# Queries reversed within each block so that bias tiles come from one row per head, a quad's sixth weight split placed behind a bank's copy, and the last four squares spaced

## The chip, the cores and the metric

The kernel runs on one core of a Trainium2 chip. The metric is the device time of one execution in microseconds. Before the change it is 1312.29 us, the median of three runs (1311.63 to 1313.32). The core's engines run side by side: TensorE (PE) multiplies matrices, with the loading of its stationary operand shown apart as PEld; VectorE (DVE) and ScalarE (ACT) do arithmetic on tiles; GpSimd (POOL) does a little arithmetic and issues DMAs that add into their target; SyncE (SP) issues most of the other DMAs. A name such as ACTq or SPq in the profile stands for the instructions by which an engine issues DMAs or waits.

## The reference, cut to what matters

One decoder layer on 512 rows of 1024 numbers: a feed-forward network (FFN), a mixer with an SSD part and a differential-attention part, cross attention into 256 memory rows, a second FFN, and a last norm.

```python
x = x + 0.5 * swiglu(rms_norm(x, norm_ffn1_w), ffn1_w_in, ffn1_w_out)     # d_ff = 2816
x = x + hybrid_mixer(rms_norm(x, norm_mix_w), ...)
x = x + memory_cross_attention(rms_norm(x, norm_cross_w), rms_norm(mem, norm_mem_w), ...)
x = x + 0.5 * swiglu(rms_norm(x, norm_ffn2_w), ffn2_w_in, ffn2_w_out)
return rms_norm(x, norm_final_w)

# in the mixer, for each of 8 attention heads and each block of 128 queries:
rel = k_pos[None, :] - q_pos[:, None]
bias = rel_bias[rel_bucket(rel)]            # depends on the distance alone
logits = einsum(q_blk, k) * scale + bias    # two maps, c = 0 and 1
logits = where(rel <= 0, logits, -inf)
w = softmax(logits[c=0]) - lam * softmax(logits[c=1])
out = w @ v
```

The bias of a query and a key depends only on their distance, so a head has one row of 512 biases, followed by masked places.

## The kernel before, in words

All large products are made in a form that keeps float32 accuracy: each operand is cut into a high part (a copy on ACT, line 155, output `wh` for weights) and a low part (a subtraction on DVE, line 156, output `wl`), and a product is three matmuls, high by high, high by low and low by high.

The two FFNs use a Strassen-like scheme. A *quad* (`quad`, line 252) makes a block of the hidden layer from seven weights, called here by their names in the code, in the order in which they are used: m1, t, t2, m2, m7, m3, t4. Each weight meets one combination of the activations in a product of 24 matmuls. The products go to three PSUM banks: "11" to `qa`, S1 to `qe`, S2 to `qb` (on top of a copy of `qa`), "12" to `qa`, S3 to `qb`, S4 to `qe`, "22" to `qb`. Between S2 and S3 the bank `qb` has to be read: line 302 copies it to `u` on ACT, and line 303 subtracts `u` from `qe` on DVE. S3 can't write the bank before the copy has read it. The quad's results are then turned into a gate (lines 450 to 453: a multiplication by the norm's `row`, a sigmoid-like function on ACT, two products into `th`).

FFN1 and FFN2 each run in thirds, of 6, 8 and 8 blocks of hidden columns (two blocks to a quad). In the second and third third of FFN1 there are eight quads whose weights t2 and t4 are summed on DVE (lines 297 and 300) while t and m7 are summed by a POOL DMA that adds into the tile (line 251). The eleven quads of FFN2 take sums that were made earlier in DRAM. The first quad of FFN2 is `fresh`: the last part of its activations arrives late, so its first two products are done in another order. After each third, `out_blocks` multiplies the `th` results by the second weight matrix into three pairs of banks (`oa`, `oe`, `ob`, matmuls of line 1300). In FFN1 its weights, too, are sums: first t1 is fetched by SP (line 1281) and added to by POOL (line 1320), then t2 = t1 + a fetched tile on DVE (line 1330), and so on. Two of the sums of the last third go into a spare tile named `gate`.

Weight tiles sit in rings: six for the fetched weights (`wr`), three each for `wh` and `wl`, four PSUM banks for the products. A fetch can start when the tile it will overwrite has been read.

The order of work has three layers. The code is emitted by an `Order` object, which holds a clock (`od.t`, advanced by each matmul), the dense work, and chains that are started at given clock values. SP and POOL then run their instructions in the order of the code. PE, ACT and DVE are reordered by a scheduler in the framework, which places an instruction by its own forecast of times; `with behind([ins]):` tells it that what is issued inside must come after a given instruction.

Between the FFNs lies the middle of the kernel. For each of the eight attention heads `queries_keys` projects queries into a bank `pq` (512 columns, one for each query) and splits them (`split("q", ...)`, lines 159 and 160, outputs `qh` and `ql`), does the same for the keys, and asks for the head's bias tile one head ahead (`ask_bias`, line 738). `scores` multiplies queries by keys and adds the bias in one DVE operation (line 776). At the end of a head, its output is transposed into a bank `pot` and split to `yah` and `yal`, with a multiplication by `wsub`; `out_attn` reads these later.

The bias tile is 128 x 512: its row p must be the head's bias row, moved by p places. Before the change the kernel writes for each head an expanded copy in DRAM, `rel_z` (128 rows of 641, 320 KB), by `expand_bias` (line 640; two on ACT's queue in `prepare`, six on SP's queue in `queries_keys`), and reads the tile from it with a step of 640, one less than a row.

Ahead of FFN2, `turn(0)` and `turn(1)` transpose the activations, copying eight tiles on ACT. Each tile is also squared and summed on ACT (`squared`, line 554). `row_from` makes the norm's row from the eight sums, by small operations on DVE and POOL and a matmul. The gate of a quad needs that row; its matmuls don't.

Of the kernel before, what the change touches and what calls it, by code (L numbers as in the profile page):

```python
# [11 lines left out]
F32 = mybir.dt.float32  # L12
# [88 lines left out]
def body(tc, a, dbg=None):  # L101
# [130 lines left out]
    def add_product(ps, w, xs, which, first, ks=None):  # L232

        wh, wl = w
        n = len(xs)
        for f in range(2):
            out = ps[:, f * H : (f + 1) * H]
            for kp in ks or range(n):
                wc = slice((f * n + kp) * P, (f * n + kp + 1) * P)
                xh, xl = xs[kp][which]  # L240
                for j, (a_, b_) in enumerate(((wh, xh), (wh, xl), (wl, xh))):
                    od.t += (H + 32) / 2400
                    newest_mm[:] = [nc.tensor.matmul(out, a_[:, wc], b_, start=first and f == 0 and kp == 0 and j == 0, stop=kp == n - 1 and j == 2, skip_group_check=True).ins]  # L243
                yield
# [15 lines left out]
    def quad(xs, src, ready, fresh=False):  # L260
# [38 lines left out]
        if not ready:  # L299
            V.tensor_tensor(t4, t2, m2, ALU.add)  # L300
        u2 = s2("u2")
        S.activation(u2, b_ps, AF.Copy)  # L302
        V.tensor_tensor(e_ps, e_ps, u2, ALU.subtract)
        yield from add_product(a_ps, split_w(m2), xs, "12", False)
        w7 = split_w(m7)
# [2 lines left out]
        yield from add_product(b_ps, w7, xs, S3, False)  # L308
        c22 = s2("c22")
        V.tensor_tensor(c22, p5, b_ps, ALU.subtract)  # L310
        yield from add_product(e_ps, split_w(m3), xs, S4, False)
        yield from add_product(b_ps, split_w(t4), xs, "22", False)
        yield (a_ps, b_ps), (e_ps, c22)

# [279 lines left out]
    wsub = cp.tile([P, 1], F32, name="wsub")  # L594
    dskh = cp.tile([P, 8], F32, name="dskh")
    rel_d = dram.tile([8, RW], F32, name="rel_d")
    rel_z = dram.tile([8, P, RW + 1], F32, name="rel_z")

    def lambdas():
        lamv = cp.tile([P, 4, 64], F32, name="lamv")  # L600
# [16 lines left out]
    def prepare():  # L617
        rel_far = small("rel_far", 64, bufs=1)[:8]
        V.memset(rel_far, MASKED)
        yield 9.0  # L620
        prel = aux("prel", (8, T))
        for i in range(2):
            mm(prel[:, i * H : (i + 1) * H], rel_sb, hot[i], True, True)
        for c in range(T, RW, 64):
            S.dma_start(rel_d[:, c : c + 64], rel_far)
        yield 1.5
        for i in range(2):
            S.activation(hot[i][:8], prel[:, i * H : (i + 1) * H], AF.Copy, scale=-8.0)
        yield 2.0
        for i in range(2):  # L630
            S.dma_start(rel_d[:, i * H : (i + 1) * H], hot[i][:8])
        hot.clear()
        yield 6.0
        for hd in range(2):
            with behind(list(recent)):
                expand_bias(S, hd)
            yield 4.0

    def expand_bias(queue, hd):
        queue.dma_start(rel_z[hd, :, :RW], rel_d[hd : hd + 1].to_broadcast([P, RW]))  # L640

    def bc_c(t):
        return t[:, None, :].to_broadcast([P, 4, 16])
# [91 lines left out]

    def ask_bias(hd):
        biases[hd] = s2("bias")
        S.dma_start(biases[hd], bass.AP(rel_z.tensor, rel_z.offset + hd * P * (RW + 1) + P - 1, [[RW, P], [1, T]]))

    def queries_keys(hd):  # L740
        if hd == 0:
            ask_bias(0)
        if hd < 7:
            ask_bias(hd + 1)
        if hd < 6:
            expand_bias(nc.sync, hd + 2)
        pq = acc("pq")
        yield from proj(pq, load_w(a["wq"][hd]), h)
        q = split("q", pq, -1.0)
        pk = acc("pk")  # L750
        yield from proj(pk, load_w(a["wk"][hd]), h)
        kq = split("k", pk)
        od.spawn(head(hd, q, kq, biases.pop(hd)), W["h0"])

    def head(hd, q, kq, bias):
# [92 lines left out]
        pt = aux("pot")  # L848
        for b in range(4):
            transpose(pt[:, b * P : (b + 1) * P], on[:, b])  # L850
        ya[hd] = split("ya", pt, wsub)
        dump(f"ya_{hd}", ya[hd][0])

    wcv = []
# [607 lines left out]
            yield from out_blocks(a[f"f2b{c}"], wsum[c], g, col4, ncol4, *((norm, store) if at_end else (None, None)), clean=c == 0)  # L1462

    def turn_last():
        yield from turn(1, summed=True)
        od.spawn(row_from(st_2, 8.0), 3.0)

    od.add(turn_last())
    od.add(ffn2())
# [89 lines left out]
```

## Time and profile before

| | |
|---|---|
| median of three runs | 1312.29 us (1311.63 to 1313.32) |
| the profiled execution | 1312.46 us |
| its span, first to last instruction | 1310.7 us (1.8 us lie outside it) |
| PE busy | 1287.7 us (98%), 7709 matmuls |
| DVE busy | 970.1 us (74%) |
| ACT busy | 707.8 us (54%) |
| POOL busy | 127.1 us (10%) |
| mean granted TensorE clock | 0.998 of full speed |
| moved by DMA | 237.38 MB, mean 181 GB/s |

Busy time is the sum of an engine's instruction times. A row of a timeline gives the start in the span, the duration, the engine, the line, the operation, the output and its inputs with their sizes; what stands in brackets is how long the engine had been idle before, and what ended the idling. In the view of waits a row reads: engine, its output and line, what it waited for; then the sum, the number of times and the longest. The duration of a matmul is drawn to a modelled end, so pace is better read from the starts: inside a quad's product the 24 matmuls start 0.12 us apart, 2.88 us for a product.

### The profile page before, as it was taken

The page shows a single profiled execution, that of the slowest core. Times are in us where ns is not written, and L with a number is a line of the kernel's source. Part 1 is how long each engine was busy: PE and PEld are TensorE (multiplying, and loading weights), DVE is VectorE, ACT ScalarE, POOL GpSimd, SP SyncE. Part 2 cuts the span into 40 slices and gives each one's busy share as a digit, 9 for nine tenths or more (in the row PEclk, how much of TensorE's full clock was granted, in tenths as well). Part 3 has the DMA queues.
Part 4 walks back from the last instruction along what each step waited for, and adds up shares of the span by engine and source line. Part 5 has one row for each costly group of instructions (what it writes and reads, how often), then busy time and mean ns, then how long its engine had stood idle before and what let it go on. Part 6 is the DMA issues. An engine that isn't in the chain of part 4 may idle for free.

```text
span 1310.7 us, 20079 instructions
## 1 busy us (share of the span) xinstructions
PE 1287.7 (98%) x7709; PEld 1123.3 (86%) x7709; DVE 970.1 (74%) x1538; ACT 707.8 (54%) x1208; POOL 127.1 (10%) x153
## 2 busy tenths in 40 slices
PE   9999999999999999999999999999999999999997
PEld 7879998997787778777788878888889999989995
DVE  6977897797775676557867686645668878877886
ACT  7545564565754564346645465434365646555564
POOL 0001010001010011101003022020001000000000
PEclk9999999999999999999999999999999999999999
DMA  9367777776984434763466548684139876656652
GB/s 339 94 171 182 203 192 212 223 200 187 291 294 146 137 65 131 256 171 105 92 185 174 177 138 239 191 222 126 66 100 272 207 232 179 189 194 180 188 200 94
DMA packets 70415, 237.38 MB, mean 181 GB/s; under 512 B 8288, under 2 KB 9792, under 8 KB 69968
## 3 DMA queue, kind: packets, MB, share of 16 engines
q1 hardware_dynamic: 54064, 182.87, 41.1%
q0 software_dynamic: 13168, 45.67, 19.4%
q10 hardware_dynamic: 3088, 7.56, 1.6%
q8 instruction: 60, 0.98, 0.3%
q14 instruction: 35, 0.29, 0.1%
HBM read 233.92 MB, written 50.91 MB: 217 GB/s over the span
## 4 chain that ended last, share of the span: by engine, by line
PE 59%; issue 11%; DVE 3%; ACT 2%; DMA 1%; POOL 1%; POOLq 0%; ACTq 0%; DVEq 0%
PE pm L146 10%; PE qb L243 8%; PE qe L243 5%; PE qa L243 5%; PE pxbc L146 4%; PE ob L1300 4%; PE pcq L146 3%; PE pz L146 3%; PE oe L1300 2%; PE oa L1300 2%; PE pcv L146 2%; PE pq L146 2%; PE pv L146 1%; PE pk L146 1%; DMA gate<-in_f1b 1%
## 5 line engine op out<-in xcount | busy, mean ns | idle before, releaser
L155 ACT ACTIVATE wh<-wr 128x1024 fp32r<-128x1024 f32 (+1 forms) x323 | 328.4, 1020 | 355.7 <-issue 75.6
L156 DVE TENSOR_TENSOR wl<-wr,wh 128x1024 fp32r<-128x1024 f32 (+1 forms) x323 | 377.8, 1173 | 142.4 <-ACT wh L155 136.1
L777 ACT ACTIVATE ec<-ec,mn 128x512 f32<-128x512 f32 (+3 forms) x64 | 35.3, 554 | 33.7 <-DVE mn L776 33.7
L146 PE MATMUL pxbc<-hnh,wh 128*128 128x512 f32 x128 | 52.6, 411 | 0.0
L146 PE MATMUL pxbc<-hnh,wl 128*128 128x512 f32 x128 | 50.2, 393 | 0.0
L146 PE MATMUL pxbc<-hnl,wh 128*128 128x512 f32 x128 | 50.2, 392 | 0.0
L243 PE MATMUL qb<-s31h,wh 128*128 128x256 f32 x152 | 43.2, 284 | 3.2 <-ACT u L302 3.2
L243 PE MATMUL qb<-s24h,wh 128*128 128x256 f32 x152 | 43.1, 284 | 1.3 <-ACT qb L287 1.3
L243 PE MATMUL qa<-h11h,wh 128*128 128x256 f32 x152 | 43.1, 283 | 0.0
L243 PE MATMUL qa<-hmh,wh 128*128 128x256 f32 x152 | 43.0, 283 | 0.0
L243 PE MATMUL qa<-hml,wh 128*128 128x256 f32 x152 | 43.0, 283 | 0.0
L243 PE MATMUL qe<-s24h,wh 128*128 128x256 f32 x152 | 43.0, 283 | 0.0
L243 PE MATMUL qe<-s24l,wh 128*128 128x256 f32 x152 | 43.0, 283 | 0.0
L243 PE MATMUL qe<-s24h,wl 128*128 128x256 f32 x152 | 43.0, 283 | 0.0
L243 PE MATMUL qb<-hmh,wh 128*128 128x256 f32 x152 | 43.0, 283 | 0.0
L243 PE MATMUL qb<-hml,wh 128*128 128x256 f32 x152 | 43.0, 283 | 0.0
L243 PE MATMUL qb<-hmh,wl 128*128 128x256 f32 x152 | 43.0, 283 | 0.0
L243 PE MATMUL qa<-h11h,wl 128*128 128x256 f32 x152 | 43.0, 283 | 0.0
L243 PE MATMUL qb<-s24l,wh 128*128 128x256 f32 x152 | 43.0, 283 | 0.0
L243 PE MATMUL qb<-s24h,wl 128*128 128x256 f32 x152 | 43.0, 283 | 0.0
L243 PE MATMUL qa<-h11l,wh 128*128 128x256 f32 x152 | 43.0, 283 | 0.0
L243 PE MATMUL qa<-hmh,wl 128*128 128x256 f32 x152 | 43.0, 283 | 0.0
(457 smaller groups left out, 4169.9 us busy)
## 6 DMA issues: line engine op xcount, KB each, us to landing
wr<-in_f2q SPq DMA_DIRECT2D x44, 512.0 KB, 4.3
wr<-in_f1q SPq DMA_DIRECT2D x40, 512.0 KB, 4.4
wr<-in_f1b SPq DMA_DIRECT2D x25, 512.0 KB, 5.3
isum<-in_f2q SPq DMA_DIRECT2D x22, 512.0 KB, 5.2
wr<-isum SPq DMA_DIRECT2D x22, 512.0 KB, 5.1
wsum<-in_f2b SPq DMA_DIRECT2D x20, 512.0 KB, 6.2
wr<-wsum SPq DMA_DIRECT2D x20, 512.0 KB, 4.7
wr<-in_f1q POOLq DMA_DIRECT2D x16, 512.0 KB, 5.9
```

The lines of the kernel that those rows point to most:

```text
L146: newest_mm[:] = [nc.tensor.matmul(out, w, x, start=start, stop=stop).ins]
L155: S.activation(hi, src, AF.Copy),
L156: V.tensor_tensor(lo, src, hi.bitcast(F32), ALU.subtract),
L243: newest_mm[:] = [nc.tensor.matmul(out, a_[:, wc], b_, start=first and f == 0 and kp == 0 and j == 0, stop=kp == n - 1 and j == 2, skip_gr ...
L777: S.activation(ec[:, :n], ec[:, :n], AF.Exp, bias=mn, scale=-1.0, accum_out=sm[c][:, i : i + 1])
L1300: newest_mm[:] = [nc.tensor.matmul(ps, a_[:, ts], b_[:, ws], start=first and k == 0 and j == 0, stop=k == n - 1 and j == 2, skip_group_che ...
```

## The change

There are three parts.

**The bias.** The expanded copy `rel_z` and its eight DMAs go. The bias tile is read from the head's single row in DRAM, with a step of one place from row to row (pattern `[[1, P], [1, T]]`). That gives the rows in the opposite order, so that the queries have to be reversed within each block of 128. This is done where the query bank is read to be split: `backwards` reads each block of 128 columns from its end to its start (a step of -1), on ACT for the high part and on DVE for the low part. The head's output then comes out reversed as well, and is put right where the bank `pot` is read to be split into `ya`, in the same way. For eight heads these are 16 reads on ACT and 16 on DVE.

**The sixth weight.** In `quad` the split of m3 is issued behind the copy of bank `qb` to `u`.

**The last squares.** `turn(1)` no longer squares its tiles. A chain of its own, `row_of_last`, started 4.0 on the clock after, issues the four squares 2.0 apart, each behind the weight split that was issued last, and then goes on to `row_from`, with 3.0 in place of 8.0 between its steps.

```diff
@@ quad
         u2 = s2("u2")
-        S.activation(u2, b_ps, AF.Copy)
+        copy = S.activation(u2, b_ps, AF.Copy)
         V.tensor_tensor(e_ps, e_ps, u2, ALU.subtract)
...
-        yield from add_product(e_ps, split_w(m3), xs, S4, False)
+        with behind([copy.ins]):
+            w3 = split_w(m3)
+        yield from add_product(e_ps, w3, xs, S4, False)
@@ prepare, queries_keys, head
-    rel_z = dram.tile([8, P, RW + 1], F32, name="rel_z")
...
-        yield 6.0
-        for hd in range(2):
-            with behind(list(recent)):
-                expand_bias(S, hd)
-            yield 4.0
-
-    def expand_bias(queue, hd):
-        queue.dma_start(rel_z[hd, :, :RW], rel_d[hd : hd + 1].to_broadcast([P, RW]))
...
-        S.dma_start(biases[hd], bass.AP(rel_z.tensor, rel_z.offset + hd * P * (RW + 1) + P - 1, [[RW, P], [1, T]]))
+        S.dma_start(biases[hd], bass.AP(rel_d.tensor, rel_d.offset + hd * RW, [[1, P], [1, T]]))
+
+    def backwards(t):
+        n = t.free_size()
+        return bass.AP(t.tensor, t.offset + P - 1, [list(t.ap[0]), [P, n // P], [-1, P]])
...
-        if hd < 6:
-            expand_bias(nc.sync, hd + 2)
...
-        q = split("q", pq, -1.0)
+        q = split("q", backwards(pq), -1.0)
...
-        ya[hd] = split("ya", pt, wsub)
+        ya[hd] = split("ya", backwards(pt), wsub)
@@ ffn2
     def turn_last():
-        yield from turn(1, summed=True)
-        od.spawn(row_from(st_2, 8.0), 3.0)
+        yield from turn(1)
+        od.spawn(row_of_last(), 4.0)
+
+    def row_of_last():
+        for k in range(4, KT):
+            with behind(list(newest)):
+                squared(k, x[k])
+            yield 2.0
+        yield from row_from(st_2, 3.0)
```

Since the scheduler sets the order on PE, ACT and DVE, small edits move instructions in other places too. The numbers in tile names count tiles, and differ by one or so between the two kernels.

The first place is ACT in the sixth of FFN1's eight quads of the second and third third. `p` is the copy of bank `qe`, `s31h` and `s24h` are high parts of activations, `wh_2802` belongs to the sixth weight (m3) and `wh_2830` to the seventh (t4), `u` is the copy of bank `qb`. Before:

```order
L295 ACTIVATE p_488_2685<-qe_2622 128x512
L155 ACTIVATE wh_2802<-wr_2614 128x1024
L155 ACTIVATE s31h_2710<-s_491_2705 128x512
L155 ACTIVATE wh_2830<-wr_2611 128x1024
L302 ACTIVATE u_495_2733<-qb_2623 128x512
L155 ACTIVATE s24h_2749<-s_492_2706 128x512
L155 ACTIVATE gh_2784<-th_2603 128x512
```

After, where m3 is `wh_2801` and t4 is `wh_2829`:

```order
L295 ACTIVATE p_488_2684<-qe_2621 128x512
L155 ACTIVATE s31h_2709<-s_491_2704 128x512
L302 ACTIVATE u_495_2732<-qb_2622 128x512
L155 ACTIVATE s24h_2748<-s_492_2705 128x512
L155 ACTIVATE wh_2801<-wr_2613 128x1024
L155 ACTIVATE gh_2783<-th_2602 128x512
L155 ACTIVATE wh_2829<-wr_2610 128x1024
```

Both weight splits stand ahead of the copy `u` before, and behind it after. In the eighth quad the same two splits stood ahead of the copy, and now stand behind it.

The second place is DVE where the sixth quad ends and the seventh begins. `gate` and `th` belong to the sixth quad's results, `c` to its third bank; `wl_2881`, `wl_2885` and `wl_2947` are the low parts of the seventh quad's m1, t and t2; the operation of line 297 makes its t2. Before:

```order
L310 TENSOR_TENSOR c_504_2800<-p_488_2685,qb_2623 128x512
L156 TENSOR_TENSOR wl_2881<-wr_2865,wh_2880 128x1024
L156 TENSOR_TENSOR wl_2885<-wr_2867,wh_2884 128x1024
L450 TENSOR_TENSOR gate_2858<-qb_2623,row_413 128x512
L297 TENSOR_TENSOR wr_2867<-wr_2867,wr_2870 128x1024
L453 TENSOR_TENSOR th_2859<-qe_2622,gate_2858 128x2x256
L453 TENSOR_TENSOR th_2859<-c_504_2800,gate_2858 128x512
L156 TENSOR_TENSOR wl_2947<-wr_2867,wh_2946 128x1024
```

After, where `wl_2830` is the sixth quad's t4, and m1, t and t2 are `wl_2880`, `wl_2884` and `wl_2946`:

```order
L310 TENSOR_TENSOR c_504_2799<-p_488_2684,qb_2622 128x512
L156 TENSOR_TENSOR wl_2830<-wr_2610,wh_2829 128x1024
L156 TENSOR_TENSOR wl_2880<-wr_2864,wh_2879 128x1024
L452 TENSOR_TENSOR gate_2857<-qb_2622,row_412 128x512
L156 TENSOR_TENSOR wl_2884<-wr_2866,wh_2883 128x1024
L297 TENSOR_TENSOR wr_2866<-wr_2866,wr_2869 128x1024
L455 TENSOR_TENSOR th_2858<-qe_2621,gate_2857 128x2x256
L455 TENSOR_TENSOR th_2858<-c_504_2799,gate_2857 128x512
L156 TENSOR_TENSOR wl_2946<-wr_2866,wh_2945 128x1024
```

The split of t now stands behind the gate's first operation instead of ahead of it, and with it the sum of line 297. On ACT at this place the copy of bank `qa` to `qb` of the seventh quad stood behind the split `wh` of t2, and now stands ahead of it.

The third place is DVE at the start of the last third's out block of FFN1. `gate` and `th` are the last quad's, `g11l` and `s31l` low parts of activations, `s` sums of them, the `wl` low parts of weights, and the two operations of line 1330 (1325 after) make the out block's t2. Before:

```order
L450 TENSOR_TENSOR gate_3381<-qb_3136,row_413 128x512
L156 TENSOR_TENSOR wl_3378<-wr_3374,wh_3377 128x1024
L156 TENSOR_TENSOR wl_3445<-wr_3442,wh_3444 128x1024
L453 TENSOR_TENSOR th_3382<-qe_3135,gate_3381 128x2x256
L453 TENSOR_TENSOR th_3382<-c_582_3310,gate_3381 128x512
L156 TENSOR_TENSOR g11l_3389<-th_3382,g11h_3388 128x256
L212 TENSOR_TENSOR s_597_3392<-th_3382 128x512
L156 TENSOR_TENSOR wl_3464<-wr_3460,wh_3463 128x1024
L213 TENSOR_TENSOR s_598_3393<-s_597_3392,th_3382 128x256
L1330 TENSOR_TENSOR wr_3374<-wr_3374,wr_3493 128x1024
L214 TENSOR_TENSOR s_598_3393<-s_598_3393,th_3382 128x256
L156 TENSOR_TENSOR s31l_3398<-s_597_3392,s31h_3397 128x512
```

After:

```order
L452 TENSOR_TENSOR gate_3380<-qb_3135,row_412 128x512
L156 TENSOR_TENSOR wl_3377<-wr_3373,wh_3376 128x1024
L455 TENSOR_TENSOR th_3381<-qe_3134,gate_3380 128x2x256
L455 TENSOR_TENSOR th_3381<-c_582_3309,gate_3380 128x512
L156 TENSOR_TENSOR g11l_3388<-th_3381,g11h_3387 128x256
L212 TENSOR_TENSOR s_597_3391<-th_3381 128x512
L156 TENSOR_TENSOR wl_3444<-wr_3441,wh_3443 128x1024
L213 TENSOR_TENSOR s_598_3392<-s_597_3391,th_3381 128x256
L156 TENSOR_TENSOR wl_3463<-wr_3459,wh_3462 128x1024
L214 TENSOR_TENSOR s_598_3392<-s_598_3392,th_3381 128x256
L156 TENSOR_TENSOR s31l_3397<-s_597_3391,s31h_3396 128x512
L1325 TENSOR_TENSOR wr_3373<-wr_3373,wr_3492 128x1024
```

The first sum of t2 has moved behind a step of the `s` sums and the low part `s31l`; the second, which followed `s31l` directly, now comes eight operations later. On ACT in the first quad of FFN2 the four squares stood together ahead of the copy of bank `qa` to `qb` (line 287), and the split `wh` of the quad's m2 behind that copy and the copy `p` of bank `qe` (line 295). Now one square and then the split of m2 stand ahead of the copy of line 287, two squares behind the copy `p`, and the last behind the copy `u`.

## The prediction

> **What bounds the kernel now.** I read the page's head first, then the waits of PE, then timelines at those waits.
>
> ```profile
> span 1310.7 us, 20079 instructions
> PE 1287.7 (98%) x7709; PEld 1123.3 (86%) x7709; DVE 970.1 (74%) x1538; ACT 707.8 (54%) x1208; POOL 127.1 (10%) x153
> ```
>
> PE is the bound. A change that leaves its matmuls alone can gain only what PE stands idle, and loses whatever new idle time it puts there. The waits say which idle time has a name:
>
> ```profile
> PE qb L243 <- ACT u L302: 3.2, 2, 1.6
> PE ob L1300 <- DVE wl L156: 2.4, 3, 1.3
> PE qb L243 <- ACT qb L287: 1.3, 1, 1.3
> ```
>
> The first row is the wait at which the weight's part of the change aims (two places, 1.6 us each), the third the wait at which the spaced squares aim, the second lies in the last out block of FFN1, which the reordering touches. Together they are 6.9 us, 0.5% of the span; the bias part touches none of them. So the question is how much of 4.5 us goes, and what new idling the moved instructions make.
>
> **The sixth weight: the two waits for `u`.** This is the timeline of FFN1's sixth quad:
>
> ```profile
> 251.30 0.61 ACT L155 ACTIVATE s31h<-s 128x512 fp32r<-128x512 f32 x1
> ...
> 252.97 0.28 PE L243 MATMUL qa<-hmh,wl 128*128 128x256 f32 x1
> 253.22 1.06 ACT L155 ACTIVATE wh<-wr 128x1024 fp32r<-128x1024 f32 x1 [1.31 <-PE qa L243]
> 254.19 0.58 ACT L302 ACTIVATE u<-qb 128x512 f32<-128x512 f32 x1
> 254.82 0.39 PE L243 MATMUL qb<-s31h,wh 128*128 128x256 f32 x1 [1.58 <-ACT u L302]
> ```
>
> The split at 253.22 is the seventh weight's (the sixth's ran before `s31h`). It waits for product "12" to end (its last matmul starts at 252.97), because the ring of three has no free `wh`; the copy `u`, queued behind it, could have run during "12". So S3 starts at 254.82, where the pace of 0.12 a matmul puts it at 253.09: 1.73 lost. After the change only `s31h` stands ahead of the copy. S2 ends 2.88 before "12" does, near 250.1; with 0.61 for `s31h` and 0.58 for the copy, `u` is ready by about 251.5, 1.6 us early. The eighth quad has the same shape:
>
> ```profile
> 292.48 1.06 ACT L155 ACTIVATE wh<-wr 128x1024 fp32r<-128x1024 f32 x1 [0.49 <-PE qb L243]
> 295.11 0.28 PE L243 MATMUL qa<-hmh,wl 128*128 128x256 f32 x1
> 295.43 0.69 DVE L450 TENSOR_TENSOR gate<-qa,row 128x512 f32<-128x512 f32 x1 [0.43 <-PE qa L243]
> 296.97 0.39 PE L243 MATMUL qb<-s31h,wh 128*128 128x256 f32 x1 [1.58 <-ACT u L302]
> ```
>
> It loses 296.97 - 295.23 = 1.74. Both go, 3.5 by starts (3.2 by the waits' row, which leaves out the wake-up; I take 3.4). What is late next is the sixth weight itself, now split after the copy. In the eighth quad its low part stands behind three half-size operations on DVE, from 295.43 on: 3 x 0.60 + 1.22 gives 298.45, while S4's third matmul (S3's start 295.23 + 2.88 + 0.24) wants it at 298.35: 0.1 lost. Sum **-3.3**. In the other seventeen quads the copy already ran in time, and the weight, free to be split during S3 (2.88 us, against 1.06 + 1.22), costs 0; without that cover it would be up to 1.2 a quad.
>
> **The spaced squares: the wait for the copy `qb`.**
>
> ```profile
> 976.62 0.62 ACT L554 ACTIVATE junk<-x 128x512 f32<-128x512 f32 x1
> ...
> 977.38 0.28 PE L243 MATMUL qa<-h11h,wl 128*128 128x256 f32 x1
> ...
> 979.07 0.58 ACT L287 ACTIVATE qb<-qa 128x512 f32<-128x512 f32 x1
> ```
>
> Four squares from 976.62 hold the copy until 979.07; it could have run at 977.38 + 0.25 = 977.63 (0.25 is the wake-up between the rows 252.97 and 253.22). If it ran then, 1.44 would be won. But in the order after, the split of m2 has come to stand ahead of it, and this split needs a `wh` that product "11" frees at the same 977.63; it takes 0.97 start to start, and the copy follows at 978.60. Won: 979.07 - 978.60 = **-0.5**; the ends are -0.4 and -1.3 (the whole wait, if the split finds its tile free earlier). The norm's row comes later, since its four squares and their matmul do (39 matmuls by the order, 4.7 us at 0.12):
>
> ```profile
> 987.67 0.60 ACT L410 ACTIVATE row<-nrow 128x512 f32<-128x512 f32 x1 [0.91 <-PE nrow L146]
> 994.85 0.69 DVE L450 TENSOR_TENSOR gate<-qb,row 128x512 f32<-128x512 f32 x1 [0.63 <-PE qb L243]
> ```
>
> From the row's end at 988.3 to the last operation of that gate, which waits for PE's last bank, there are 6.6 us, so that the delay is covered: 0, and 1 for 1 beyond.
>
> **The turn from the sixth to the seventh quad: a new wait.** DVE and ACT now take the second weight and the copy in another order. Before:
>
> ```profile
> 263.75 0.69 DVE L450 TENSOR_TENSOR gate<-qb,row 128x512 f32<-128x512 f32 x1 [0.63 <-PE qb L243]
> 264.36 1.22 DVE L297 TENSOR_TENSOR wr<-wr,wr 128x1024 f32<-128x1024 f32 x1
> ...
> 266.79 1.23 DVE L156 TENSOR_TENSOR wl<-wr,wh 128x1024 fp32r<-128x1024 f32 x1
> ...
> 269.55 0.28 PE L243 MATMUL qb<-s24h,wl 128*128 128x256 f32 x1
> ```
>
> The rows are the gate, the sum t2, t2's low part, and the matmul that first needs it: 269.55 - 268.02 = 1.5 us of slack. t's low part ran before the gate. After, it comes behind the gate, at 264.36, and takes 1.2, so that the sum is done at 266.8; on ACT the copy of `qa` then goes first (0.52), about 267.3 to 267.85, the split of t2 ends near 268.9, its low part near 270.2. That is 0.65 after 269.55, and about a quarter of a microsecond more follows in "12", whose weight is behind it: **+0.9**. Ends: 0 (the copy comes at once, and the sum is not late) and +1.2 (one more weight operation's 1.22 in the way).
>
> **The last out block.** Timeline rows, one row of the chain of work that ended last (the 13.17), and a row of the DMA view, from 320 to 342 us in 40 slices:
>
> ```profile
> 312.38 1.22 DVE L1330 TENSOR_TENSOR wr<-wr,wr 128x1024 f32<-128x1024 f32 x1
> 313.63 0.33 SPq L1281 DMA_DIRECT2D wr<-in_f1b  x1
> ...
> 334.96 0.50 PE L1300 MATMUL ob<-wl,s31h 128*128 128x512 f32 x1 [0.53 <-DVE wl L156]
> ```
>
> ```profile
> 319.31 13.17 DMA gate<-in_f1b
> ```
>
> ```profile
> DMA  7799999999999999999999999999999999732779
> ```
>
> SP's fetch at 313.63 waits for the sum of line 1330; behind it are POOL's sum, which lands at 319.31 + 13.17 = 332.48, and the products of 334.96. After, the sum comes behind a 128x512 and a 128x256 operation more: 0.69 (the gate's rows above) + about 0.4 = 1.1 later. Against that stand the DMA engines, full until about 339 (the nines): there a transfer's end is set by what is queued, not by when it was asked, and one `rel_z` expansion less is in the queue. This is its price and the bias tile's row:
>
> ```profile
> q10 hardware_dynamic: 3088, 7.56, 1.6%
> L738 ACTq DMA_DIRECT2D bias<-rel_z x8: 326/326/582, 372.6 to 589.2; - x8
> L776 DVE CUSTOM_DVE_ANT_0 ec<-ps,bias x64: 282/486/693, 391.2 to 641.5; 128x512 f32<-128x512 f32 x16, 128x384 f32<-128x384 f32 x16, 128x256 f32<-128x256 f32 x16, 128x128 f32<-128x128 f32 x16
> ```
>
> Queue 10 took 1.6% of 1310.7 = 21 us for 7.56 MB, so 0.32 MB take 0.9 us of all engines. Ends are therefore +1.1 and -0.9, or -1.8 if both expansions of this stretch count; I take the middle, **-0.3**. The bias tile's own read costs 0: it is asked at 372.6 and first used at 391.2.
>
> **The reversed reads.** No instruction before steps backwards. The reads that change, and the nearest pair, a plain copy and a copy that writes four places apart:
>
> ```profile
> L159 ACT ACTIVATE qh<-pq x8: 575/582/594, 381.9 to 620.2; 128x512 fp32r<-128x512 f32 x8
> L160 DVE SCALAR_TENSOR_TENSOR ql<-pq,qh x8: 680/683/689, 383.2 to 622.3; 128x512 fp32r<-128x512 f32 x8
> ...
> L159 ACT ACTIVATE yah<-pot,wsub x8: 669/677/690, 430.1 to 663.3; 128x512 fp32r<-128x512 f32 x8
> L160 DVE SCALAR_TENSOR_TENSOR yal<-pot,wsub,yah x8: 744/748/751, 430.8 to 664.0; 128x512 fp32r<-128x512 f32 x8
> ...
> L699 DVE COPY cum<-pcum x1: 217/217/217, 407.4 to 407.4; 128x64 f32<-128x64 f32 x1
> L706 DVE COPY by_hd<-cum x1: 217/217/217, 408.0 to 408.0; 128x64 f32<-128x64 f32 x1
> ```
>
> The two copies take the same 217 ns: the step cost nothing there. So **0** is nearest; the far end is a doubling, 8 x (0.58 + 0.68 + 0.68 + 0.75) = 21.5 us of engine time, most of it beside the key projection (24 matmuls) and, for `ya`, long before `out_attn`. Below nothing I see no way.
>
> The Trainium skill speaks against this part. Its page "Vector Engine (DVE) Microarchitecture Reference", section "5.2 Measured stream behaviour on trn2 (trn3 not measured)", has a port stream at full rate only in runs of at least two adjacent words, and gives 1.7 to 2.5 ns a column instead of 1.05 where every element hops; the streams were in SBUF, and the page says elsewhere that a negative step was not measured. By it a 512-column DVE read would cost an estimated 0.35 to 0.75 us more, 5.6 to 12 us over sixteen of them, and the sum would be anywhere from the forecast to that much above it. The copy that writes four places apart shows no such price in this trace.
>
> **Sum.** -3.3 - 0.5 + 0.9 - 0.3 + 0 = -3.2. The profiled execution's 1312.46 becomes 1309.26; it stands 0.17 above the median, so **1309.1**. About 0.2% (2.6 us) can be told from no change, that is below 1309.7 or above 1314.9.
>
> **Rivals.**
>
> *More is won.* The DMA relief ends the out block's wait (2.4 by the second row of waits) and the seventh quad finds its copy in time: -3.3 - 0.5 - 1.8 = -5.6, 1306.7. For it speak the full DMA engines; against it the order of DVE there.
>
> *The gain is eaten.* The seventh quad pays 1.2 and again in "12", 1.8 together, the out block its full 1.1, the copy of the fresh quad nothing: -3.3 + 1.8 + 1.1 = -0.4, 1311.9. For it speaks that each operation named is nearer its use than before; against it, that DVE is idle 26% and can catch up.
>
> *Slower: the reversed reads double.* Place: the splits of `q` and `ya` in the heads. It decides from 2.6 + 3.2 = 5.8 us on the path, 27% of the 21.5; at 40% the time is 1309.1 + 8.6 = 1317.7. The trace's 217 ns pair and the covers speak against it.
>
> *Slower too: a late load in the eighth quad.* POOL's sum for m7 gets its tile about 2 us later. In
>
> ```profile
> L251 POOL DMA_DIRECT2D wr<-in_f1q x1: 866/866/866, 280.8 to 280.8; - x1
> ...
> DMA to landing us min/median/max: 8.1/8.1/8.1
> ```
>
> it lands at 288.9, and its split starts at 292.48: 3.6 us of cover, so 0 in the sum. If the transfer falls among others and lands 6 us later still, the kernel ends near 1315.
>
> **Chances and range.** The forecast, 1307.6 to 1310.8: 0.50, 0.40 of it faster by over 0.2%. More won, 1305.8 to 1307.6: 0.16. Eaten, 1310.8 to 1313: 0.19. Reads: 0.10. Late load: 0.05. So faster 0.56, same 0.29, slower 0.15. The range 1306.6 to 1313.0 leaves out the slower cases and a little of the case above: under 2 in 10.
>
> **What would show it.** Right: no row of PE waiting for `u` at line 302, a wait of about 0.9 for line 287, a new wait of 0.6 to 0.9 for `wl` of line 156 in bank `qb` near 268 us; `qh` near 582 ns and `yal` near 748; the out block's waits near 2.4. Wrong: those reads clearly longer with DVE or ACT waited for by the score matmuls, or a wait for a DMA ahead of S3 in the eighth quad.

## The result, and the profile after

The changed kernel takes 1310.86 us (median of 21 runs, 1308.14 to 1314.11), the kernel before, run beside it, 1313.04 us (21 runs, 1311.27 to 1314.07). The ratio is 0.9986 with a 95% interval of 0.9981 to 0.9992: 1.1 to 2.5 us faster, in the range, but two thirds of the 3.2 us that were forecast. Run again beside the experiments it took 1310.52 us against 1312.25, a ratio of 0.9989 (0.9980 to 0.9998).

The profiled execution of the changed kernel took 1313.05 us, 2.2 above its median, so its span must not be set against the one of before. This is the head of its page, and a row of the view by stretches (start and end; length; PE's busy time and matmuls; granted clock; share and rate of the DMA engines):

```profile
span 1311.3 us, 20085 instructions
...
PE 1290.0 (98%) x7709; PEld 1124.1 (86%) x7709; DVE 970.7 (74%) x1538; ACT 707.7 (54%) x1208; POOL 126.4 (10%) x153
```

```profile
330.00:338.00 8.00, 6.91 (x22) 0.79 1.08 294
```

The mean granted clock of these 8 us was 0.79: for about 3.5 us it was 0.50 or so, which cost PE an estimated 1.7 us (by stretches of 1 us, 332 to 336: 0.53, 0.50, 0.50, 0.77). A second profile, of the run called after_again below, has no such dip; its span is 1309.1 us, and its execution took 1310.9, near the median. I use the first for what lies ahead of the out block, the second for the rest. The waits of PE in the first profile, the rows that answer to those of before:

```profile
PE ob L1295 <- ACT wh L155: 2.1, 2, 1.1
...
PE ob L1295 <- DVE wl L156: 0.9, 2, 0.5
...
PE oe L1295 <- DVE s31l L156: 0.9, 2, 0.7
...
PE qb L243 <- ACT qb L287: 0.8, 1, 0.8
```

The row of `u` (3.2) is gone, the copy of the fresh quad waits 0.8 in place of 1.3, and the out blocks have new rows: `wh` grew from 0.8 to 2.1, and `oe` waits for `s31l`, which it never did before. The sixth quad did what was forecast:

```profile
250.14 0.63 ACT L155 ACTIVATE s31h<-s 128x512 fp32r<-128x512 f32 x1 [1.41 <-DVE s L212]
250.68 0.58 ACT L302 ACTIVATE u<-qb 128x512 f32<-128x512 f32 x1
...
251.67 1.05 ACT L155 ACTIVATE wh<-wr 128x1024 fp32r<-128x1024 f32 x1
...
252.69 0.28 PE L243 MATMUL qa<-hmh,wl 128*128 128x256 f32 x1
252.81 0.28 PE L243 MATMUL qb<-s31h,wh 128*128 128x256 f32 x1
```

The copy runs at 250.68, with product "12" still on PE, and S3 follows "12" at the pace of 0.12. The weight is split after it.

**Where the time went.** The order of the matmuls is nearly the same in both kernels, so the start of the n-th matmul can be compared from profile to profile. To read where PE loses time, I took each interval between the starts of two matmuls, less the usual interval of that shape, and added those more than 0.2 us too long, by place. The last two rows need no such threshold: they say how much earlier than in before the same matmul starts, at before's 304 and 340 us, which are the two ends of the third out block. All values are us of the profiled executions (the third out block of "after" holds the dip above):

| PE's lost time at | before | w3_alone | after | after_again | w3_6_8 | before_no_sums | after_no_sums |
|---|---|---|---|---|---|---|---|
| second out block of FFN1, 184 to 200 us | 0 | 1.4 | 1.2 | 0 | 0 | 0 | 0 |
| the copies `u`, and S4 of the eighth quad | 3.5 | 0 | 0 | 0.8 | 0 | 3.5 | 0 |
| third out block of FFN1, 304 to 340 us | 2.6 | 4.5 | 6.0 | 3.5 | 3.0 | 0 | 0 |
| first quad of FFN2 | 1.5 | 1.5 | 1.0 | 1.0 | 1.0 | 1.5 | 1.0 |
| PE ahead of before at 304 us | 0 | 1.6 | 3.3 | 2.6 | 3.1 | 0.2 | 3.2 |
| PE ahead of before at 340 us | 0 | -0.6 | -1.2 | 1.1 | 2.5 | 3.4 | 6.4 |

(The columns are the kernels of the experiments below.) The 3.5 us of the copies are won in every kernel with the edit, and a large part is handed back in the two out blocks, where the weights are late. One profile of a kernel is a small sample here: squares_alone and bias_alone, whose code up to this block's end has before's order, lose 1.6 and 1.5 us in the third out block where before loses 2.6, and "after" was 1.6 us ahead at 100 us already, ahead of any edited quad.

### The profile page after: what moved, and what is told of

The parts are those of the page before. It is cut to its first block, busy times and chain, and to the rows that moved or that the text cites. A ratio compares the mean times of both kernels' runs of the same rounds, so it can differ in the third digit from the quotient of the medians.

```text
span 1311.3 us, 20085 instructions
## 1 busy us (share of the span) xinstructions
PE 1290.0 (98%) x7709; PEld 1124.1 (86%) x7709; DVE 970.7 (74%) x1538; ACT 707.7 (54%) x1208; POOL 126.4 (10%) x153
## 4 chain that ended last, share of the span: by engine, by line
PE 75%; issue 14%; DVE 4%; DMA 4%; ACT 2%; POOL 2%; POOLq 0%; ACTq 0%; DVEq 0%
PE qb L243 11%; PE pm L146 10%; PE qa L243 8%; PE qe L243 7%; PE ob L1295 5%; PE pxbc L146 4%; PE oa L1295 3%; PE pcq L146 3%; PE oe L1295 3%; PE pz L146 3%; DMA wr<-in_f1b 2%; PE pcv L146 2%; PE pg L146 2%; PE pu L146 2%; PE pa L146 2%
## 5 line engine op out<-in xcount | busy, mean ns | idle before, releaser
L243 PE MATMUL qb<-s31l,wh 128*128 128x256 f32 x152 | 43.0, 283 | 0.0
L243 PE MATMUL qb<-s31h,wl 128*128 128x256 f32 x152 | 43.0, 283 | 0.0
```

## The experiments

Four theories were held against each other. Theory 1: the terms of the forecast stand. Theory 2: the lead won at the copies is lost where FFN1's summed weights come late. Theory 3: the weight's part is worth nothing, and the gain is the bias part's. Theory 4: the lead is lost by the order of DVE in the last out block.

### The three parts alone, and the changed kernel again

Each part by itself on the kernel before. The first, w3_alone:

```diff
-        S.activation(u2, b_ps, AF.Copy)
+        copy = S.activation(u2, b_ps, AF.Copy)
...
-        yield from add_product(e_ps, split_w(m3), xs, S4, False)
+        with behind([copy.ins]):
+            w3 = split_w(m3)
+        yield from add_product(e_ps, w3, xs, S4, False)
```

> The kernel before with the sixth weight's split placed behind the copy u, and nothing else. Theory 1 (the terms of the forecast stand): the two waits for u (3.5 us by starts) are gone, the turn from the sixth to the seventh quad costs 0.3 to 0.9, and the last out block of FFN1 stays near its 2.6 us of waits: 2.5 to 3 us faster than before. Theory 2 (the lead is given back where the loads of FFN1's last out block set the pace): the two waits are gone just the same, but the waits for wh and wl between the end of the eighth quad and the end of that block grow from 2.6 to 4 us or more, and the whole is only 0.5 to 1.5 us faster. Theory 3 (the weight's edit is worth nothing, the gain is the bias part's): within 0.4 us of before.

Measured: 1313.13 us against 1312.25, ratio 1.0008 (0.9999 to 1.0017). The edit that was to bring 3.3 us brings nothing by itself. In its profile the two waits are gone (the table's 0), so the term's place was right; the time that theory 1 drew from it was not. Theory 2 said the direction, though it had the loss too small, and the time itself is nearest to theory 3's "within 0.4 us".

The second, squares_alone (`turn_last` and `row_of_last` of the change):

```diff
     def turn_last():
-        yield from turn(1, summed=True)
-        od.spawn(row_from(st_2, 8.0), 3.0)
+        yield from turn(1)
+        od.spawn(row_of_last(), 4.0)
```

> The kernel before with the last four squares spaced, and nothing else; its order differs only in the first quad of FFN2. Theories 1 and 2: PE's wait for the copy qb at the first quad of FFN2 is 0.8 in place of 1.3, and the kernel is 0.5 us faster, no other wait changes. Theory 3: no difference of the time beyond 0.3 us.

Measured: 1311.57 us, ratio 0.9995 (0.9986 to 1.0004). The time can't be told from no change; in its profile the wait is 0.8 in place of 1.3, and the next matmuls come 0.5 us earlier than in before at that place.

The third, bias_alone (no `rel_z`, the bias read from `rel_d`, `backwards` on the two reads):

```diff
-        q = split("q", pq, -1.0)
+        q = split("q", backwards(pq), -1.0)
...
-        ya[hd] = split("ya", pt, wsub)
+        ya[hd] = split("ya", backwards(pt), wsub)
```

> The kernel before with the reversed queries and the bias tiles from one row, without the other two edits; the order on PE, DVE and ACT is that of before but for the DMAs that are gone. Theory 1: the reads take what they took (qh 582 ns, ql 683, yah 677, yal 748), the DMA engines are relieved by 0.9 us of work near 324 us, and the kernel is 0 to 0.5 us faster. Theory 2: the same, since the last out block's loads are asked before the expansions. Theory 3: 1.5 to 2 us faster, by shorter waits at FFN1's last out block.

Measured: 1311.94 us, ratio 0.9997 (0.9988 to 1.0006): theory 3, by which this part brings 1.5 to 2 us, falls. The three parts alone add up to no change (+0.0008, -0.0005 and -0.0003, each give or take 0.0009), and the whole kernel gains 0.0011 to 0.0014; the intervals don't say whether the parts help one another. In the profile of the changed kernel the reversed reads are:

```profile
L159 ACT ACTIVATE qh<-pq x8: 573/582/592, 383.1 to 621.5; 128x512 fp32r<-128x512 f32 x8
L160 DVE SCALAR_TENSOR_TENSOR ql<-pq,qh x8: 680/684/690, 384.4 to 623.5; 128x512 fp32r<-128x512 f32 x8
...
L159 ACT ACTIVATE yah<-pot,wsub x8: 672/678/690, 431.3 to 664.5; 128x512 fp32r<-128x512 f32 x8
L160 DVE SCALAR_TENSOR_TENSOR yal<-pot,wsub,yah x8: 745/749/752, 432.0 to 665.2; 128x512 fp32r<-128x512 f32 x8
```

The medians are 582, 684, 678 and 749 ns, against 582, 683, 677 and 748: a step of -1 costs nothing on either engine.

The changed kernel once more, after_again:

> The changed kernel once more, for a second profile and for its time beside the three parts on one chip. Theory 1: a profile without the dip of the granted clock shows the out block's waits back at about 2.6 us and the span near 1307.5. Theory 2: the waits between 305 and 335 us are 4 us or more in this profile too, and the time is 1.5 to 2.5 below before. Theory 3: as bias_alone to within 0.5 us.

Measured: 1310.52 us, ratio 0.9989 (0.9980 to 0.9998). Without the dip of the clock the third out block still loses 3.5 us by the table. Theory 2 had said 4 or more, theory 1 2.6; the number lies between them. What it waits for says more. These are ACT's rows there, in before and in after_again, a split of t1's second part, and how long that part's POOL sum took to land:

```profile
308.47 1.06 ACT L155 ACTIVATE wh<-wr 128x1024 fp32r<-128x1024 f32 x1 [0.68 <-ACT gate L451]
```

```profile
DMA to landing us min/median/max: 8.2/8.2/8.2
```

```profile
305.93 0.40 ACT L155 ACTIVATE g11h<-th 128x256 fp32r<-128x256 f32 x1
309.50 1.06 ACT L155 ACTIVATE wh<-wr 128x1024 fp32r<-128x1024 f32 x1 [3.17 <-DMA wr<-in_f1b]
310.47 0.62 ACT L155 ACTIVATE s31h<-s 128x512 fp32r<-128x512 f32 x1
```

```profile
DMA to landing us min/median/max: 9.8/9.8/9.8
```

PE comes to this place 2.6 us earlier than before, and the load comes 2.8 us later (issued at 299.61 in place of 298.44, landing after 9.8 in place of 8.2). ACT stands 3.17 us, and `s31h`, DVE's low parts and the sum of line 1325 stand behind it in their queues:

```profile
310.60 1.23 DVE L156 TENSOR_TENSOR wl<-wr,wh 128x1024 fp32r<-128x1024 f32 x1 [1.73 <-ACT wh L155]
...
312.67 1.22 DVE L1325 TENSOR_TENSOR wr<-wr,wr 128x1024 f32<-128x1024 f32 x1
...
318.25 1.22 DVE L1325 TENSOR_TENSOR wr<-wr,wr 128x1024 f32<-128x1024 f32 x1
```

```profile
320.62 0.50 PE L1295 MATMUL ob<-wh,s24h 128*128 128x512 f32 x1 [1.07 <-ACT wh L155]
```

Before, the first sum began at 312.38 and the second at 314.46. Here the second, at 318.25, comes with seven operations between it and the first, as read in the order, and PE's wait of 1.07 is for its split. DVE runs from 310.60, where the late split let it go on, to the end of the second sum without a pause, so that the 1.73 us that it stood for the load are in the second sum's time as well as the order is. So in absolute time the block's work begins where it began, and the lead is gone: this matmul starts at 320.62 here, and the same one at 320.67 in before. In the rest of the block before loses more, and at 340 us 1.1 of the 2.6 us are back.

### The sums left out

To take the loads' delay away with the same products, the POOL sums into t and m7 of FFN1's eight quads, and into t1 of its out blocks, are left out of both kernels; the tiles then hold one summand.

```diff
-            t, m3, m2, m7 = raw_w(b12, b11), raw_w(b22), raw_w(b21), raw_w(b12, b22)
+            t, m3, m2, m7 = raw_w(b12), raw_w(b22), raw_w(b21), raw_w(b12)
...
-            t_raw[part] = added(blocks[B12], blocks[B11])(part)
+            t_raw[part] = fetch(blocks[B12], part)
```

> The changed kernel without the POOL sums into t and m7 of FFN1's eight quads and into t1 of its out blocks: those weights are fetched, and what should be added to them is left out, so that the output is another one, with the same matmuls. Theory 2 (the lead from the u waits is lost because loads come late: the sixth weight's tile is released later, the next quad's m7 is fetched and summed later, and with it the out block's t1): no split of ACT waits for a DMA between 284 and 312 us, the lead of about 3.4 us lives on past the last out block, and this kernel is 3 to 4.5 us below the one named before_no_sums. Theory 4 (the lead is lost by the order of DVE in the out block: the sums of line 1325 stand behind other operations): the lead is lost at the same place, and the kernel is 1 to 2 us below before_no_sums, as the changed kernel is below the kernel before.

> The kernel before with the same sums left out, as the other half of the comparison. Both theories: the two waits for u stay (3.2 us in the view of waits), since they don't come from loads. Theory 2: otherwise it gains what its out block lost to loads, 0.5 to 2 us below before. Theory 4: within 1 us of before.

Measured: before_no_sums 1307.52 us (ratio to before 0.9966, 0.9953 to 0.9978), after_no_sums 1303.63 us (0.9938, 0.9924 to 0.9951). The difference is 3.9 us, where the kernels with their sums differ by 1.7 to 2.2. Between the two profiles PE gains 1.8 us at each of the two copies and 0.5 at the fresh quad, and loses 0.4 in its first 100 us and 0.3 in S4 of the eighth quad; nowhere else do they differ by 0.1. The waits of PE, of before_no_sums and then of after_no_sums:

```profile
PE qb L243 <- ACT u L302: 3.2, 2, 1.6
...
PE qb L243 <- ACT qb L287: 1.3, 1, 1.3
...
PE ob L1300 <- DVE wl L156: 1.1, 1, 1.1
```

```profile
PE ob L1295 <- DVE wl L156: 0.9, 1, 0.9
PE qb L243 <- ACT qb L287: 0.8, 1, 0.8
```

The one `ob` wait left is in the first out block, near 89 us; the second and third have none. With the loads out of the way the change is worth what its terms A (the copies) and B (the squares) said, 3.3 + 0.5 = 3.8. One thing the leaving out did beside: the scheduler, which counts on earlier loads, put the sums of t2 in the third out block earlier on DVE, in both kernels (the first ahead of `th` in before_no_sums and right behind it in after_no_sums, the second right behind `s31l`, where before has it anyway). So this pair shows that loads and what is ordered by them eat the lead, and doesn't part theory 2 from theory 4 in the third block. The kernel before also wins 4.7 us by the missing sums, more than the 0.5 to 2 expected. Of the 5.3 us between the two spans 3.1 lie in the third out block, where its loads held it too. 1.8 lie behind the last matmul, which starts 9.7 us ahead of the span's end in before and in after_again, and 7.9 us ahead of it in both kernels without the sums; why is not shown, and since both have it the comparison isn't touched.

### The edit in two quads alone

```diff
+    quads = [0]
+
     def quad(xs, src, ready, fresh=False):
+        quads[0] += 1
+        late = quads[0] in (6, 8)
...
-        with behind([copy.ins]):
+        with behind([copy.ins] if late else []):
             w3 = split_w(m3)
```

> The changed kernel with the sixth weight's split behind the copy u in the sixth and eighth quad alone, where the copy was late; in all other quads the split stands where it stood before the change. Theory 2: the seventh quad releases its m3 tile as early as before, the eighth quad's m7 is in place by about 289 us and its split waits for no DMA, the out block's t1 comes earlier too, and the kernel is 1 to 2 us below the changed one. Theory 4: the order of DVE in the out block is that of the changed kernel, so the time is within 0.5 us of it.

Measured: 1308.58 us against 1312.24, ratio 0.9974 (0.9963 to 0.9984), the fastest of the kernels that keep all their sums, and 1.6 to 2.0 us below the changed kernel by the ratios (0.9986 and 0.9989; the intervals overlap a little). The time is as theory 2 said; its reason is not. DVE's order in the third out block is that of the changed kernel, so theory 4 doesn't give this gain. The split of the eighth quad's m7 still waited 2.8 us for its load, and the third out block lost 3.0 us, less than the 3.5 or more of the kernels with the edit in all quads. What is gone is the loss in the second out block: there the edit in the first four quads, where no copy was late, had cost time and could win none. In the changed kernel ACT waits there for t1's second part; in before, the same split waits for PE only:

```profile
185.33 1.06 ACT L155 ACTIVATE wh<-wr 128x1024 fp32r<-128x1024 f32 x1 [1.55 <-DMA wr<-in_f1b]
```

```profile
185.65 1.06 ACT L155 ACTIVATE wh<-wr 128x1024 fp32r<-128x1024 f32 x1 [0.29 <-PE oa L1300]
```

Of six profiles of kernels with the edit in those quads and with the sums, five lose 0.8 to 2.7 us in the second out block; of the eight others, none loses more than 0.5. The size is not typical: these five executions took 0.4 to 3.7 us more than the medians of their kernels. DVE's order in that block is the same with the edit and without, so that here the load alone is late: with the edit t1's second sum takes 8.4 to 10.7 us from issue to landing and lands at 184.8 to 188.4 us, in the six profiles with the sums and without the edit 5.4 to 8.8, and it lands at 183.9 to 185.4.

The edit left out of the seventh quad alone, w3_not7 (`late = quads[0] != 7`):

> The changed kernel with the sixth weight's split left where it was in the seventh quad alone; the order differs from the changed kernel's by two rows on ACT and three on DVE, all in that quad. Theory 2: the seventh quad's m3 tile is released 0.4 us earlier or more, m7 follows, and the kernel is 0.4 to 2 us below the changed one; if the whole gain of w3_6_8 is to be had from this quad, near 1308.6. Theory 4: within 0.5 us of the changed kernel.

Measured: 1311.00 us, ratio 0.9992 (0.9983 to 1.0000), no better than the changed kernel; its profile (of an execution 2.0 us above the median) loses 1.6 us in the second out block and 4.4 in the third. So the seventh quad is not what w3_6_8 won.

### The eighth quad's m7 fetched earlier

The profile of after_again had an ACT split waiting 3.8 us for m7, and t1's second part is fetched behind that split. The swap gives m7 an earlier tile:

```diff
-            t, m3, m2, m7 = raw_w(b12, b11), raw_w(b22), raw_w(b21), raw_w(b12, b22)
+            t, m3, m7, m2 = raw_w(b12, b11), raw_w(b22), raw_w(b12, b22), raw_w(b21)
```

> The changed kernel with one swap: in FFN1's eight quads m7 (a fetch and a POOL sum) is fetched ahead of m2 (a fetch alone), so that it gets the tile that comes free about 4 us earlier. The order on PE, DVE and ACT is the same, row by row. Theory 2, now with its link named (the eighth quad's m7 is fetched behind the seventh quad's m3, lands at 290.7 where its split stood ready near 287, and the out block's t1 is fetched behind m7's split): m7 lands by 288, its split waits less than 1 us in place of 3.8, t1's second part is fetched before 292 in place of 293.1, and the kernel is 1 to 2.5 us below the changed one. Theory 4 (the order of DVE in the out block): within 0.5 us of the changed kernel.

> The same swap on the kernel before. Theory 2: there m7 landed at 288.9 and its split began at 289.6 because a tile came free then, so the load did not hold it; 0 to 0.7 us below before. If it wins as much as on the changed kernel, the swap is a gain of its own and says nothing on the lead.

> The kernel named w3_6_8 with the same swap. Theory 2: 0.5 to 2 us below w3_6_8, the fastest so far, near 1307. Theory 4: as w3_6_8, near 1308.6.

Measured: m7_early 1311.49 us (ratio 1.0000, 0.9990 to 1.0010), m7_early_before 1312.98 (1.0008, 0.9999 to 1.0016), m7_early_w3 1309.74 (0.9987, 0.9978 to 0.9995). None wins; each stands above its pair without the swap, within the intervals. m7_early and m7_early_w3 differ by the edit in the other quads, and by 1.7 us, as the changed kernel and w3_6_8 do. ACT's waits for loads, in after_again (262 to 312 us) and in m7_early (262 to 322; an execution of 1315.2 us, 3.7 above the median):

```profile
ACT wh L155 <- DMA wr<-in_f1q: 3.8, 1, 3.8
ACT wh L155 <- DMA wr<-in_f1b: 3.2, 1, 3.2
```

```profile
ACT wh L155 <- DMA wr<-in_f1b: 3.9, 1, 3.9
```

The swap does cure the first wait, and the second, t1's, grows. The link that I had named, that m7 holds up t1, doesn't bring the time: t1's second sum takes 9.6 us in m7_early as in the changed kernel, and in m7_early_w3, where it is asked 1.45 us earlier than in w3_6_8 (299.52 in place of 300.97), it takes 8.9 in place of 8.0. Theory 4 had these times right. But the trace shows ACT waiting 3.9 us for a load at this place, ahead of what DVE's order holds up; both have a share in the third block, and these runs don't part them.

### The second weight of the fresh quad behind the copy

```diff
-                S.activation(b_ps, a_ps, AF.Copy)
+                base = [S.activation(b_ps, a_ps, AF.Copy).ins]
...
-        yield from add_product(a_ps, split_w(m2), xs, "12", False)
+        with behind(base if fresh else []):
+            w2 = split_w(m2)
+        yield from add_product(a_ps, w2, xs, "12", False)
```

> The changed kernel with the split of m2 in the first quad of FFN2 issued behind the copy of qa to qb. All theories: PE's wait for that copy, 0.8 us in the changed kernel, goes nearly to nothing (under 0.2), since the copy then runs at the end of product 11; 0.6 to 0.9 us below the changed kernel, unless the later m2 makes product 12 wait. Before the out block nothing differs.

Measured: 1311.29 us, ratio 0.9989 (0.9981 to 0.9998), the same ratio as after_again. In its profile the wait for the copy is gone and PE wins 0.8 us at that place against after_again, but 0.8 us is lost again in products near 1030 us, where an ACT split waits 4.1 us for a load, a wait that after_again doesn't have. The time doesn't tell it from the changed kernel, and whether that loss belongs to the edit is open.

## Why the prediction was right or wrong

**The copies `u`, -3.3: right in place and size.** 3.5 us by starts are gone in each profile with the edit, and 3.5 remain in each without. The eighth quad's S4 waits at its third matmul, as read, for 0.25 us in place of 0.1.

**The squares, -0.5: right, and for the reason given.** From after_again:

```profile
976.54 1.06 ACT L155 ACTIVATE wh<-wr 128x1024 fp32r<-128x1024 f32 x1 [0.25 <-PE qa L243]
977.50 0.58 ACT L287 ACTIVATE qb<-qa 128x512 f32<-128x512 f32 x1
```

The split waits for product "11", and the copy stands behind it; 0.5 is won out of 1.5, and the later row of the norm held nobody.

**The seventh quad, +0.9: too large.** The first profile has 0.3, in "12" alone:

```profile
261.65 0.69 DVE L452 TENSOR_TENSOR gate<-qb,row 128x512 f32<-128x512 f32 x1 [2.80 <-PE qb L243]
262.26 1.22 DVE L156 TENSOR_TENSOR wl<-wr,wh 128x1024 fp32r<-128x1024 f32 x1
263.51 1.23 DVE L297 TENSOR_TENSOR wr<-wr,wr 128x1024 f32<-128x1024 f32 x1
...
266.11 1.23 DVE L156 TENSOR_TENSOR wl<-wr,wh 128x1024 fp32r<-128x1024 f32 x1 [0.17 <-ACT wh L155]
```

The order was as read, but t2's low part follows the sum by 1.4 us (264.74 to 266.11), where I had it 2.1 later (266.8 to 268.9): the copy `qb` had run before the sum was done.

**The other seventeen quads, 0, the eighth quad's m7, 0, and the last out block, -0.3: wrong, and here the forecast failed.** Three errors are in it. The smallest is m7's. I gave it a cover of 3.6 us, from its landing at 288.9 to a split at 292.48; but that split is m3's. m7's is three rows earlier in before:

```profile
289.60 1.06 ACT L155 ACTIVATE wh<-wr 128x1024 fp32r<-128x1024 f32 x1 [1.00 <-PE qe L243]
```

Its cover was 0.7 us, and in after_again the same split, due about 1.7 us earlier on PE's count, starts at 290.78 after 3.82 us of waiting. Curing m7 alone won nothing, so the larger part lies in the other two.

The second error is the 0 for the other seventeen quads. I priced the sixth weight's later split there by whether the weight itself had time for S4, and left out that its tile is released later, and with it the fetches behind it. Leaving the edit out of the quads without a late copy gave back 1.6 to 2.0 us. What was lost at the second out block can't come from a lead, since PE has none yet from the copies there. The eleven quads of FFN2 cost nothing: behind its first quad PE's lead over before stays the same to 0.1 us in w3_alone and in "after".

The third is that every cover was read on the clock of the kernel before. A lead of 3.4 us shortens by 3.4 us the cover of each load that is asked at a time which the lead doesn't move. The DMA rows held such loads (the sums land 8 us after they are asked, and ACT's splits follow within 2). Its size is read from the third out block of the two kernels with the edit in two quads alone: PE's lead goes there from 3.1 to 2.5 us in w3_6_8 and from 3.3 to 2.2 in m7_early_w3, while three more profiles of kernels without the edit gain -0.1 to 1.2 us on before in the same block. In the kernels without the edit t1's second sum of the third block lands after 7.2 to 8.2 us; with it in all quads after 8.7 to 9.8. That the summed weights, and what is ordered by them, hand the gain back is shown, since without these sums all of it stays. Two things stay open: why a sum takes longer (the times of issue suggest several transfers at once, and no run isolates it), and in the third block the share of DVE's order, which put the second sum late.

**The relief of the DMA engines, part of the same -0.3: not seen.** bias_alone is at 0.9997, with an interval that holds both 0 and the 0.9.

**The reversed reads, 0: right,** and the rival by which they double is out. By the estimate from the page of the Trainium skill named in the prediction, "Vector Engine (DVE) Microarchitecture Reference", section "5.2 Measured stream behaviour on trn2 (trn3 not measured)", a read would take 0.35 to 0.75 us more if its rule for hopping single words reached these; here the difference is 1 ns. The rows are of PSUM, the page's of SBUF, so this bounds how far the rule carries rather than refutes it. The pair of 217 ns that the prediction held against the rule was weak evidence: one of the two copies reads PSUM and the other SBUF, 64 columns each.

**The cases.** The measured -2.2 lies between the forecast and the rival "the gain is eaten" (-0.4), which had the right place, the out block, and at most a part of the cause, the order of DVE. Taken as a time, 1310.86 us lies just inside that rival's case, which began at 1310.8. By the bound of 0.2% the result counts as no change, to which I gave 0.29, and not as faster, to which I gave 0.56. So the time came into the range with the two gains right and the losses wrong, one of them too large and the other too small: +0.9 at the seventh quad, where 0.3 was lost, and 0 or less at the loads, where the kernels without the sums put the whole loss at 1.7 to 2.2 us. That the two errors partly cancel is luck. The rival "a late load in the eighth quad", to which I gave 0.05, came true in its mechanism and not in its price. In after_again m7's split waits 3.8 us for its load, the sixth weight's split runs behind it, and S4 waits:

```profile
297.48 0.39 PE L243 MATMUL qe<-s24h,wl 128*128 128x256 f32 x1 [0.62 <-DVE wl L156]
```

That is 0.8 us by the table, where I had priced about 6.

## What to carry to other kernels

A cover read from a profile holds on that profile's clock: when an edit lets the bound engine come earlier, subtract the gain from the cover of everything downstream that the edit doesn't move, loads above all, before adding gains up. An edit that frees a waiting instruction by moving another one back also moves back the release of what that one reads; put it only where the wait is, since in the places without one it can only cost. And to test whether loads eat a gain, leave a part of the loads out of both kernels and compare the difference, not the times: the loads that are left out may win something of their own.

## What the runs showed of the hardware

- Reading a PSUM bank backwards, in blocks of 128 of 512 columns, costs the same as forwards on ACT (582 and 678 ns against 582 and 677) and on DVE (684 and 749 against 683 and 748).
- A POOL DMA that adds 512 KB into a tile landed between 5.4 and 10.7 us after its issue at the same place of the program (t1's second part in the second out block, over twelve profiles of kernels that keep the sums), so that a cover of a microsecond or two before such a load is none.
- Without these sums the spread of the runs shrank: 1303.29 to 1304.41 and 1307.20 to 1307.94 over five runs each, against 1311.21 to 1314.21 over the seventeen runs of before beside them.
